# Dense mixture-of-experts dispatch: all loads ahead of the entry barrier, and four stores in place of five

## The chip, the cores and the metric

The kernel runs on one core of one Trainium2 chip. The metric is the time of one execution on the device in microseconds (us). The kernel before takes 92.71 us, the median of three runs (92.69 to 92.94). The profiled execution that is read below took 92.44 us, and its span, from the first recorded instruction to the last, is 90.7 us; times inside the kernel are counted from the start of that span.

## The reference

```python
batch, seq_len, d_model, n_experts = 8, 256, 512, 8
x             # (8, 256, 512) float32
gate_weights  # (8, 256, 8)   float32, not negative

def reference(x, gate_weights):
    gate_weights = gate_weights / (np.sum(gate_weights, axis=-1, keepdims=True) + 1e-8)
    output = x[:, :, None, :] * gate_weights[:, :, :, None]
    return output.astype(np.float32)
```

Each of the 2048 tokens has 512 numbers and 8 gate weights. The weights of a token are divided by their sum, and the token is written out eight times, each time multiplied by one of them. 4.19 MB of x and 0.07 MB of gates are read, 33.55 MB are written: the output is eight times as large as x.

## The kernel before

The 2048 tokens are laid out as 128 partitions with 16 tokens each (j from 0 to 15). So "a token" below means one j: 128 rows of 512 numbers for x, 128 rows of 8 x 512 numbers (16 KB in a partition) for the output. The results of one token fill one slot of a ring of ten slots; five stores, all issued by SyncE, write them out.

```python
SLOTS = 10
HEAD = 2
TAIL = 13
CHUNKS = ((0, 2, 0), (2, 3, 2), (5, 3, 5), (8, 4, 0), (12, 4, 6))   # first token, tokens, first slot

# ... issue_before_entry_barrier(nc, loads): moves the named loads to the front of their
#     engine's program, ahead of the barrier at which all engines meet at entry

    first_loads = [
        nc.sync.dma_start(out=g_all, in_=g_v),                                    # gates
        nc.scalar.dma_start(out=x_all[:, 0:HEAD, :], in_=x_v[:, 0:HEAD, :]),      # two tokens
    ]
    issue_before_entry_barrier(nc, first_loads)
    body_load = nc.sync.dma_start(
        out=x_all[:, HEAD:TAIL, :], in_=x_v[:, HEAD:TAIL, :]                      # eleven tokens
    )
    nc.sync.dma_start(out=x_all[:, TAIL:J, :], in_=x_v[:, TAIL:J, :])             # three tokens

    nc.vector.memset(warm, 0.0)
    nc.scalar.copy(out=warm, in_=warm)

    nc.vector.reduce_sum(out=gsum, in_=g_all, axis=mybir.AxisListType.X)
    nc.vector.tensor_scalar_add(out=gsum, in0=gsum, scalar1=1e-8)
    nc.vector.reciprocal(out=gsum, in_=gsum)
    nc.vector.tensor_tensor(
        out=gn, in0=g_all, in1=gsum.to_broadcast([P, J, E]), op=mult
    )

    # ... scale_one(engine, j, e, slot): one token times one gate, on ScalarE or VectorE (512 a partition)
    # ... scale_token(j, slot): one token times its eight gates, one VectorE instruction (4096 a partition)

    for j0, m, s0 in CHUNKS:
        for i in range(m):
            j, slot = j0 + i, s0 + i
            if j < 2:
                for e in range(E):
                    on_act = e < 3
                    scale_one(nc.scalar if on_act else nc.vector, j, e, slot)
            elif j == 2:
                for e in range(E):
                    scale_one(nc.scalar, j, e, slot)
            elif j == 3:
                for e in range(E):
                    scale_one(nc.scalar if e < 2 else nc.vector, j, e, slot)
            elif i == 0:
                for e in range(E):
                    scale_one(nc.scalar, j, e, slot)
            else:
                scale_token(j, slot)
        store = nc.sync.dma_start(
            out=out_v[:, j0 : j0 + m, :, :], in_=ring[:, s0 : s0 + m, :, :]
        )
        if j0 == 0:
            tc.add_manual_dep(
                store.ins,
                body_load.ins.name,
                # ...
                reason="no store among the loads",
            )
```

The slots 0 to 3 and 6 to 9 are used a second time, by the tokens 8 to 11 and 12 to 15: their scalings wait until the store that reads the slot has landed.

Of the kernel before, what the change touches and what calls it, by code (L numbers as in the profile page):

```python
# [1 line left out]

# [4 lines left out]

SLOTS = 10
HEAD = 2
TAIL = 13  # L10
CHUNKS = ((0, 2, 0), (2, 3, 2), (5, 3, 5), (8, 4, 0), (12, 4, 6))


def issue_before_entry_barrier(nc, loads):
    names = [bi.ins.name for bi in loads]

    def move(nc):
        blocks = nc.main_func.blocks
        entry = blocks[0].instructions
        moved = []  # L20
        for block in blocks[1:]:
            for ins in list(block.instructions):
                if ins.name in names:
                    block.instructions.remove(ins)
                    moved.append(ins)
        assert sorted(i.name for i in moved) == sorted(names)
        for ins in moved:
            at = next(k for k, other in enumerate(entry) if other.engine == ins.engine)
            entry.insert(at, ins)

    nc.at_finalize(move)


@with_exitstack
def kernel(
    ctx: ExitStack,
    tc: tile.TileContext,
    x: bass.AP,
    gate_weights: bass.AP,
    out: bass.AP,  # L40
):
    nc = tc.nc
    P = 128

    B, S, D = x.shape
    E = gate_weights.shape[-1]
    J = B * S // P

    fp32 = mybir.dt.float32
    mult = mybir.AluOpType.mult  # L50

    x_v = x.flatten_outer_dims().rearrange("(p j) d -> p j d", p=P)
    g_v = gate_weights.flatten_outer_dims().rearrange("(p j) e -> p j e", p=P)
    out_v = out.rearrange("b s e d -> (b s) e d").rearrange(
        "(p j) e d -> p j e d", p=P
    )

    pool = ctx.enter_context(tc.tile_pool(name="pool", bufs=1))

    g_all = pool.tile([P, J, E], fp32)  # L60
    x_all = pool.tile([P, J, D], fp32)
    ring = pool.tile([P, SLOTS, E, D], fp32)
    gsum = pool.tile([P, J, 1], fp32)
    gn = pool.tile([P, J, E], fp32)
    warm = pool.tile([P, 1], fp32)

    first_loads = [
        nc.sync.dma_start(out=g_all, in_=g_v),
        nc.scalar.dma_start(out=x_all[:, 0:HEAD, :], in_=x_v[:, 0:HEAD, :]),
    ]  # L70
    issue_before_entry_barrier(nc, first_loads)
    body_load = nc.sync.dma_start(
        out=x_all[:, HEAD:TAIL, :], in_=x_v[:, HEAD:TAIL, :]
    )
    nc.sync.dma_start(out=x_all[:, TAIL:J, :], in_=x_v[:, TAIL:J, :])

    nc.vector.memset(warm, 0.0)  # L77
    nc.scalar.copy(out=warm, in_=warm)  # L78
# [8 lines that stand above are left out]
    def scale_one(engine, j, e, slot):  # L87
        o_ap, s_ap = ring[:, slot, e, :], gn[:, j, e : e + 1]
        if engine is nc.scalar:
            nc.scalar.mul(out=o_ap, in_=x_all[:, j, :], mul=s_ap)  # L90
        else:
            nc.vector.tensor_scalar_mul(out=o_ap, in0=x_all[:, j, :], scalar1=s_ap)  # L92

    def scale_token(j, slot):
        nc.vector.tensor_tensor(  # L95
            out=ring[:, slot, :, :],
            in0=x_all[:, j : j + 1, :].to_broadcast([P, E, D]),
            in1=gn[:, j, :].unsqueeze(2).to_broadcast([P, E, D]),
            op=mult,
# [6 lines that stand above are left out]
                for e in range(E):  # L106
                    on_act = e < 3
                    scale_one(nc.scalar if on_act else nc.vector, j, e, slot)
            elif j == 2:
                for e in range(E):  # L110
                    scale_one(nc.scalar, j, e, slot)
            elif j == 3:
                for e in range(E):
                    scale_one(nc.scalar if e < 2 else nc.vector, j, e, slot)
            elif i == 0:
                for e in range(E):
                    scale_one(nc.scalar, j, e, slot)
            else:
                scale_token(j, slot)
        store = nc.sync.dma_start(  # L120
            out=out_v[:, j0 : j0 + m, :, :], in_=ring[:, s0 : s0 + m, :, :]
        )
        if j0 == 0:
            tc.add_manual_dep(
                store.ins,
                body_load.ins.name,
                mybir.DependencyInfo(
                    mybir.DependencyClass.Sync, mybir.DependencyReason.DATA
                ),
                reason="no store among the loads",  # L130
            )


# [1 line left out]
_INS = ['x', 'gate_weights']  # L135
_OUTS = [((8, 256, 8, 512), 'float32')]


# [23 lines left out]
```

## Time and profile before

| | |
|---|---|
| time, median of 3 runs | 92.71 us |
| span of the profiled execution | 90.7 us |
| VectorE busy | 46.7 us, 52% |
| ScalarE busy | 26.4 us, 29% |
| scaling of one token by one gate on ScalarE (40 of them) | 708 ns each |
| the same on VectorE (16) | 482 ns each |
| scaling of one token by all eight gates on VectorE (9) | 4420 ns each |
| mean rate of all transfers over the span | 417 GB/s |

A "busy" share is an average over the whole span, and its instructions overlap a little where they follow each other, so that ten VectorE scalings of 482 ns take 4.05 us. A transfer shows up in three places: the instruction that issues it, in the timeline of the issuing queue (some 0.35 us); its packets, which are moved by 16 DMA engines and are counted in the DMA row and by queue; and its landing, on which other instructions wait. The issuing queues of SyncE and ScalarE are called SPq and ACTq in the profile, and their packets are booked under q1 and q10. One packet is here one partition's part of a transfer.

### The profile page before, as it was taken

Reading aid. Unit: us, or ns where it says so; the run is one execution under the profiler, and the core shown is the slowest. Engines: PE = TensorE matmul, PEld = TensorE weight load, DVE = VectorE, ACT = ScalarE, POOL = GpSimd, SP = SyncE. Lnnn points to the kernel's source line nnn. Section 1 sums busy time; section 2 is a strip of 40 time slices with the busy share of each in tenths; the row PEclk is TensorE's granted clock in tenths of the full one; section 3 lists DMA queues with packets and bytes.
Section 4 is the critical chain, followed back from the end, with each engine's and each line's share of the span. In section 5 each row is a group of like instructions: output and inputs, shape, how many; then the busy total and the mean of one; then the engine's idle time right before and its main releaser. Section 6 shows DMA issues by size and latency. Waiting matters only on the chain.

```text
span 90.7 us, 140 instructions
## 1 busy us (share of the span) xinstructions
DVE 46.7 (52%) x30; ACT 26.4 (29%) x42; POOL 0.2 (0%) x4
## 2 busy tenths in 40 slices
DVE  0795399999999999999990495000000000000000
ACT  5393399997990000000000497000000000000000
POOL 0000000000000000000000000000000000000000
DMA  4998999999898889888988999999999982999990
GB/s 110 468 467 378 383 536 463 463 390 419 347 694 347 347 347 694 347 347 347 694 347 347 463 463 463 463 463 463 463 463 463 463 347 116 463 463 463 463 463 0
DMA packets 1296, 37.81 MB, mean 417 GB/s; under 512 B 144, under 2 KB 272, under 8 KB 528
## 3 DMA queue, kind: packets, MB, share of 16 engines
q1 hardware_dynamic: 1152, 37.29, 95.5%
q10 hardware_dynamic: 144, 0.52, 1.6%
HBM read 4.26 MB, written 33.55 MB: 417 GB/s over the span
## 4 chain that ended last, share of the span: by engine, by line
DMA 38%; DVE 17%; ACT 5%; ACTq 1%; issue 0%; SPq 0%
DMA out_dram<-ring 28%; DVE ring L95 14%; DMA x_all<-in_x_dram 11%; ACT ring L90 5%; DVE ring L92 3%; ACTq L157 1%; ACTq L90 0%; SPq L120 0%
## 5 line engine op out<-in xcount | busy, mean ns | idle before, releaser
L95 DVE TENSOR_TENSOR ring<-x_all,gn 128x4096 f32<-128x4096 f32 x9 | 39.2, 4420 | 3.5 <-DMA out_dram<-ring 3.5
L90 ACT ACTIVATE ring<-x_all,gn 128x512 f32<-128x512 f32 x40 | 24.9, 708 | 28.8 <-DMA out_dram<-ring 24.5
L92 DVE TENSOR_SCALAR ring<-x_all,gn 128x512 f32<-128x512 f32 x16 | 6.5, 482 | 2.8 <-DMA x_all<-in_x_dram 2.8
L78 ACT ACT_TABLE_LOAD x1 | 1.3, 1283 | 0.9 <-PEq L146 0.9
L80 DVE TENSOR_REDUCE gsum<-g_all 128x16 f32<-128x128 f32 x1 | 0.3, 286 | 1.6 <-DMA g_all<-in_gate_weights_dram 1.6
L77 DVE MEMSET warm<- 128x1 f32 x1 | 0.1, 59 | 1.0 <-PEq L146 1.0
L83 DVE TENSOR_TENSOR gn<-g_all,gsum 128x128 f32<-128x128 f32 x1 | 0.3, 291 | 0.0
L82 DVE RECIPROCAL gsum<-gsum 128x16 f32<-128x16 f32 x1 | 0.3, 252 | 0.0
L78 ACT COPY warm<-warm 128x1 f32<-128x1 f32 x1 | 0.2, 191 | 0.0
L81 DVE TENSOR_SCALAR gsum<-gsum 128x16 f32<-128x16 f32 x1 | 0.2, 176 | 0.0
L146 POOL MEMSET const-bfloat16-1.0<- 128x1 bf16 x1 | 0.1, 102 | 0.0
L146 POOL MEMSET const-uint8-127<- 128x1 uint8 x1 | 0.1, 102 | 0.0
L146 POOL MEMSET const-float32-0.0<- 128x1 f32 x1 | 0.1, 99 | 0.2 <-issue 0.2
L146 POOL MEMSET const-float32-1.0<- 128x1 f32 x1 | 0.1, 99 | 0.0
## 6 DMA issues: line engine op xcount, KB each, us to landing
out_dram<-ring SPq DMA_DIRECT2D x2, 6144.0 KB, 22.1
out_dram<-ring SPq DMA_DIRECT2D x1, 4096.0 KB, 11.5
x_all<-in_x_dram SPq DMA_DIRECT2D x1, 2816.0 KB, 9.6
x_all<-in_x_dram SPq DMA_DIRECT2D x1, 768.0 KB, 11.1
x_all<-in_x_dram ACTq DMA_DIRECT2D x1, 512.0 KB, 3.7
g_all<-in_gate_weights_dram SPq DMA_DIRECT2D x1, 64.0 KB, 2.6
out_dram<-ring SPq DMA_DIRECT2D x2, 28.1
```

The source lines that it names most:

```text
L77: nc.vector.memset(warm, 0.0)
L78: nc.scalar.copy(out=warm, in_=warm)
L80: nc.vector.reduce_sum(out=gsum, in_=g_all, axis=mybir.AxisListType.X)
L81: nc.vector.tensor_scalar_add(out=gsum, in0=gsum, scalar1=1e-8)
L82: nc.vector.reciprocal(out=gsum, in_=gsum)
L83: nc.vector.tensor_tensor(out=gn, in0=g_all, in1=gsum.to_broadcast([P, J, E]), op=mult)
L90: nc.scalar.mul(out=o_ap, in_=x_all[:, j, :], mul=s_ap)
L92: nc.vector.tensor_scalar_mul(out=o_ap, in0=x_all[:, j, :], scalar1=s_ap)
L95: nc.vector.tensor_tensor(out=ring[:, slot, :, :], in0=x_all[:, j : j + 1, :].to_broadcast([P, E, D]), in1=gn[:, j, :].unsqueeze(2).to_bro ...
L146: nc = _bacc.Bacc("TRN2", target_bir_lowering=False, num_devices=1)
L157: with _tile.TileContext(nc) as tc:
```

## The change

All three loads are now issued ahead of the entry barrier: first four tokens of x and then the other twelve from SyncE, and the gates from ScalarE. With every load issued before any store in the same queue, the explicit wait of the first store for the load of eleven tokens is dropped. The four stores have 2, 4, 4 and 6 tokens; the last reuses the slots 0 to 5. The work of the tokens 2 to 5 is dealt anew between the two engines, and ScalarE takes the tokens 6, 10, 11 and 12 whole. The aim is to have the engines that move the data supplied from the very beginning, with fewer and larger transfers, and never to let them run out between loads and stores.

```diff
-HEAD = 2
-TAIL = 13
-CHUNKS = ((0, 2, 0), (2, 3, 2), (5, 3, 5), (8, 4, 0), (12, 4, 6))
+HEAD = 4
+CHUNKS = ((0, 2, 0), (2, 4, 2), (6, 4, 6), (10, 6, 0))
 # ...
-        for ins in moved:
+        for ins in reversed(moved):
             at = next(k for k, other in enumerate(entry) if other.engine == ins.engine)
             entry.insert(at, ins)
 # ...
-    first_loads = [
-        nc.sync.dma_start(out=g_all, in_=g_v),
-        nc.scalar.dma_start(out=x_all[:, 0:HEAD, :], in_=x_v[:, 0:HEAD, :]),
-    ]
-    issue_before_entry_barrier(nc, first_loads)
-    body_load = nc.sync.dma_start(
-        out=x_all[:, HEAD:TAIL, :], in_=x_v[:, HEAD:TAIL, :]
-    )
-    nc.sync.dma_start(out=x_all[:, TAIL:J, :], in_=x_v[:, TAIL:J, :])
+    first_load = nc.sync.dma_start(out=x_all[:, 0:HEAD, :], in_=x_v[:, 0:HEAD, :])
+    gate_load = nc.scalar.dma_start(out=g_all, in_=g_v)
+    last_load = nc.sync.dma_start(out=x_all[:, HEAD:J, :], in_=x_v[:, HEAD:J, :])
+    issue_before_entry_barrier(nc, [first_load, gate_load, last_load])
 # ...
-            elif j == 2:
+            elif j < 6:
+                on_act = (8, 4, 0, 0)[i]
                 for e in range(E):
-                    scale_one(nc.scalar, j, e, slot)
-            elif j == 3:
-                for e in range(E):
-                    scale_one(nc.scalar if e < 2 else nc.vector, j, e, slot)
-            elif i == 0:
+                    scale_one(nc.scalar if e < on_act else nc.vector, j, e, slot)
+            elif j in (6, 10, 11, 12):
                 for e in range(E):
                     scale_one(nc.scalar, j, e, slot)
             else:
                 scale_token(j, slot)
-        store = nc.sync.dma_start(
+        nc.sync.dma_start(
             out=out_v[:, j0 : j0 + m, :, :], in_=ring[:, s0 : s0 + m, :, :]
         )
-        if j0 == 0:
-            tc.add_manual_dep(
-                # ... store.ins on body_load.ins.name, "no store among the loads"
-            )
```

More of the change, by code (lines that the diff above doesn't have):

```diff
@@ L119 @@
                 scale_token(j, slot)
-        store = nc.sync.dma_start(
+        nc.sync.dma_start(
             out=out_v[:, j0 : j0 + m, :, :], in_=ring[:, s0 : s0 + m, :, :]
         )
-        if j0 == 0:
-            tc.add_manual_dep(
[L125 to L130, printed above, removed]
-            )
 _INS = ['x', 'gate_weights']
```

## The prediction

> **What bounds the kernel now.** I read the page's second and third parts first, then the DMA issues, then SyncE's own waits, then the first microseconds of the timeline. The second part of the page (40 slices of 2.27 us each):
>
> ```profile
> DVE  0795399999999999999990495000000000000000
> ACT  5393399997990000000000497000000000000000
> ...
> DMA  4998999999898889888988999999999982999990
> ```
>
> The DMA row is full from the second slice to the last but one. VectorE and ScalarE have nothing to do after slice 25 of 40. The dips to 8 and 2 come from how whole packets are dealt to slices: counted packet by packet in the trace, all 16 DMA engines have work without a break from about 2.25 us on. The third part says how much there is:
>
> ```profile
> DMA packets 1296, 37.81 MB, mean 417 GB/s; under 512 B 144, under 2 KB 272, under 8 KB 528
> q1 hardware_dynamic: 1152, 37.29, 95.5%
> q10 hardware_dynamic: 144, 0.52, 1.6%
> ```
>
> 95.5% and 1.6% make 97.1% of 90.7 us, 88.0 us of packets for each of the 16 engines. q1 is SyncE's queue and q10 ScalarE's. The first data packet starts at 1.01 us and the last ends at 89.43 us, 88.42 us apart: only about 0.45 us per engine is idle in between, all of it in the ramp before 2.25 us. The other 2.3 us of the span are 1.0 ahead of the first packet and 1.2 behind the last one. So what the change can win is (a) part of 0.45 us, (b) per-packet costs; what it can lose is any gap that opens between the loads and the first store, or between two stores.
>
> Each store's margin is read from SyncE's waits, with the issues in the timeline at 10.60, 17.41, 26.08, 47.76 and 56.18 us:
>
> ```profile
> SPq L120 <- DVE ring L95: 43.5, 4, 21.3
> SPq L157 <- DMA out_dram<-ring: 33.1, 1, 33.1
> SPq L120 <- DMA x_all<-in_x_dram: 8.8, 1, 8.8
> ```
>
> Long as they are, these waits cost nothing: packets of the second store first move at 21.37 us, 4 us after its issue. The 8.8 us is the wait which the change removes: the first store's numbers are done at 7.96 us (ten VectorE scalings, 4.05 us from 3.91), but the store is held until the load of eleven tokens has landed.
>
> **What the Trainium skill says.** The Trainium skill, "DMA: Bandwidth & Descriptors", section "Issuing engines are not separate DMA queues": loads issued by SyncE and ScalarE run on the same 16 engines, and a second queue saves only issue time. The trace agrees: q1 and q10 fill one sum. Same page, "Queues, rings and completion order": each engine goes round-robin between rings, draining a whole packet of several descriptors from one before switching. This decides the case, and the trace agrees as far as it goes: the head of x (q10) and the eleven-token load (q1, issued at 0.91, so there from about 1.9) do not alternate. In the stretch 2.24 to 2.94 us all 66 packets are of q10, and packet by packet in the trace each of the 16 first packets of the eleven-token load starts 5 or 6 ns after one of q10's 16 completion packets:
>
> ```profile
> DMA packets 66, 0.27 MB, mean 386 GB/s; under 512 B 0, under 2 KB 0, under 8 KB 66
> ...
> q10 hardware_dynamic: 66, 0.27, 95.9%
> ```
>
> So a transfer once begun on an engine is finished there (eight packets and a completion) before the other queue has its turn. "Where 436 GB/s comes from" on the same page gives 435.2 GB/s over 16 ports, 27.2 for one; the trace's 65,536-byte packets take 2418 ns, 27.1 GB/s. A faster engine is not to be had.
>
> **The change part by part.** Packet times first, from the trace's medians: 6,144 bytes 234 ns and 22,528 bytes 836 ns, so 0.0367 ns a byte plus 8.3 ns. (Check: 4,096 bytes gives 159, measured 159; 65,536 gives 2416, measured 2418.)
>
> *Bytes and packets.* Every engine serves 8 partitions. Before: gates 8 x 27, head 8 x 159, eleven tokens 8 x 836, three tokens 8 x 234, stores 8 x 1213, 16 x 1815, 16 x 2418 = 87.5 us; measured 88.0, the rest being slow first reads (about 0.4 us above the medians in the loads) and completion packets. After: gates 8 x 27 = 0.22; four tokens, 8,192 bytes, 8 x 309 = 2.48; twelve tokens, 24,576 bytes, 8 x 911 = 7.29; stores 9.70, 38.69, and for six tokens (98,304 bytes a partition, which I take to go as two packets of 49,152) 16 x 1815 = 29.04: 87.4 us. Saved: 0.06, and with two completion packets fewer about 0.08. Fewer stores bring nothing, since they were queued end to end.
>
> *Ahead of the barrier.* The twelve-token load is issued right behind the first (issue takes 0.33 to 0.42 us each) and is in the ring long before the four tokens are through. The first transfer has 309 ns packets in place of 27 ns gates, so engines do not run dry while the rest of the descriptors arrive: I give 0.2 of the 0.45 us ramp. The barrier itself comes some 0.4 us later, because SyncE reaches it later; ScalarE's table load then ends at 2.6 in place of 2.2 us, still ahead of the gates.
>
> *The start of the compute: later.* Now the gates stand behind four tokens. In the kernel before, the head's completion packets fall between 2.94 and 3.48 us after about 1.7 us of work on an engine, so engines effectively began at 1.24 to 1.78. After: 2.48 for the four tokens, 0.2 slow reads, 0.23 gates, so the gates' last packet at 4.15 to 4.7 us. From last packet to reader took 0.37 us (2.23 to the reduction at 2.61), so the reduction starts at about 5.05; the four small VectorE operations take 1.30 (2.61 to 3.91), then 4.05 for ten scalings: 10.4 us in place of 7.96.
>
> *The first store.* Issue 10.4, in place of 10.60; from issue to first packets 1.0 to 1.5 us (the gates' load before: issued 0.00, packets from 1.01 on): 11.4 to 11.9. Loads are gone from the engines at 1.24 to 1.78 + 2.9 + 7.3 + 0.1 = 11.55 to 12.1. So the removed wait gives nothing: the numbers arrive just as the loads run out. I expect a gap of 0 to 0.4 us, 0.1 in the mean.
>
> *The later stores.* Each is due when the one ahead drains. From 11.6: 21.3, 40.7 and 60.0 us, end near 89.1. Second store: VectorE does four scalings of token 3 (to 12.0), waits for the twelve tokens (about 12.0), does 16 for tokens 4 and 5 at 0.41 each (2.47 for 6): 18.6, packets at 19.6, 1.7 us to spare. ScalarE needs twelve at 0.62 (11.14 for 18), done at 17.5. Third: three whole tokens at 4.37 (13.01 for 3, with hand-over): 31.7, 8 to spare. Last: slots 2 to 5 come free when the second store lands at 41; three tokens on VectorE end at 54.4, packets at 55.4, 4.6 to spare. ScalarE has three tokens there, 5.0 us each, two of them long before.
>
> Sum: -0.1 packets, -0.2 ramp, +0.1 gap ahead of the first store: 92.71 - 0.2 = 92.5 us.
>
> **Rivals.** *Gates starved.* If an engine drains both x loads of SyncE's ring before it turns to ScalarE's, the gates arrive at 12.2 us instead of 5.05; the first store's packets then start at about 18.6 to 19.1, some 7 us after the loads are gone: 99.4 us. For it: both x loads are in one ring, and the trace shows no case where two transfers of one ring competed with one of another. Against: the round-robin of the Trainium skill's page, and in the trace the switch to q10 at the end of the gates' transfer. About one in twelve. *A gap ahead of the first store.* The margin worked out is nothing, and its terms (start of engines, slow first reads, issue to first packet) are uncertain by some 0.3 us each; 0.5 to 1.0 us of gap makes 93.0 to 93.5. *The second store late.* Its margin of 1.7 us is the smallest of the later ones; a late landing of the twelve tokens eats it one for one, but the same delay also pushes the first store's drain, so 93 at most. *All of the ramp won.* If gates and four tokens fill the engines at once and no gap opens, 0.45 + 0.1 + some 0.3 of slow reads are saved: 91.9. More than 2% (below 90.9) can't come from anything listed, as 37.81 MB stay.
>
> **Range and chances.** The sum is 92.5; the ramp and the gap give 91.9 to 93.4 eight times in ten, the upper side wider for the gap. Faster by over 2% 0.01; slower by over 2% (above 94.6) only by starved gates or a gap of over 2 us: 0.10; within 2% 0.89.
>
> **What would show it.** In the profile after: the reduction (L80 before) starting near 5 us shows the order of the queues; near 12 us, starvation. First store issued at 10.4. Bandwidth slices from the second on without a hole near 12 us (slice 5) and near 21 us. Sum of both queues about 87.8 us. Last store issued near 54.5. I am wrong if DMA slices have a hole after slice 1, or if the six-token store's packets are slower per byte than the others.

## Result: 92.22 us, half a per cent faster

The kernel after takes 92.22 us (median of 6 runs, 92.10 to 92.33), the kernel before 92.70 us in the same comparison; the ratio is 0.9946 with a 95% interval of 0.9931 to 0.9961. The change is a real gain of 0.5 us, well inside the 2% band. The prediction said 92.5 us with a range of 91.9 to 93.4.

The page of the kernel after, second and third part (40 slices of 2.26 us; packets, megabytes and share of 16 engines by queue):

```profile
DVE  0059989999999900006999991000000000000000
ACT  4219999999999920006950000000000000000000
...
DMA  5999999999999999867999999988998899889980
...
DMA packets 1136, 37.81 MB, mean 418 GB/s; under 512 B 112, under 2 KB 240, under 8 KB 240
q1 hardware_dynamic: 992, 37.75, 97.1%
q10 hardware_dynamic: 144, 0.07, 0.2%
```

The DMA row is again full from the second slice on. There is no hole at slice 5 or 6, where the first store follows the loads, nor at slice 9 or 10, where the second store follows the first. The 8, 6 and 7 further on are, as in the kernel before, whole packets dealt to slices; no work is missing there (0.00 us in the table below). VectorE and ScalarE start their scalings at 6.45 us, some 2.5 us or a good slice later than before. 97.3% of the 90.5 us span are 88.1 us of packets per engine, as much as before.

The timeline of the kernel after, its first 20 us (start, duration, both in us; lines left out):

```profile
0.00 0.39 SPq L66 DMA_DIRECT2D x_all<-in_x_dram  x1
0.12 0.38 ACTq L67 DMA_DIRECT2D g_all<-in_gate_weights_dram  x1
...
0.44 0.42 SPq L68 DMA_DIRECT2D x_all<-in_x_dram  x1
...
5.30 0.29 DVE L74 TENSOR_REDUCE gsum<-g_all 128x16 f32<-128x128 f32 x1 [3.90 <-DMA g_all<-in_gate_weights_dram]
...
6.45 5.63 DVE L86 TENSOR_SCALAR ring<-x_all,gn 128x512 f32<-128x512 f32 x14
10.58 44.57 SPq L112 DMA_DIRECT2D out_dram<-ring  x4
12.48 6.42 DVE L86 TENSOR_SCALAR ring<-x_all,gn 128x512 f32<-128x512 f32 x16 [0.40 <-DMA x_all<-in_x_dram]
```

The reduction of the gates starts at 5.30 us (2.61 before), since the gates now share the engines with four tokens of x, and yet the first store is issued at 10.58 us, where it was issued at 10.60 before. Packet by packet in the trace, the engines end the twelve tokens between 11.43 and 12.05 us and begin the first store at most 36 ns later, most of them after 2 or 3: no gap.

SyncE's own waits in the kernel after (us in total, times, longest):

```profile
SPq L112 <- DVE ring L89: 35.0, 2, 22.4
SPq L140 <- DMA out_dram<-ring: 34.4, 2, 28.9
SPq L112 <- DVE ring L86: 17.3, 2, 9.3
```

The wait of 8.8 us for the load is gone, and a wait of 9.3 us for VectorE's scalings has taken its place.

Counted over the packets of both traces, in us per engine:

| | before | after |
|---|---|---|
| first packet starts / last packet ends | 1.01 / 89.43 | 1.02 / 89.36 |
| sum of packets | 88.02 | 88.15 |
| without work, from the first packet to 4 us | 0.44 | 0.24 |
| without work, 4 to 85 us | 0.01 | 0.00 |

So these two executions differ by 0.1 us only (92.44 and 92.33 us), a fifth of the gain in the medians. The other four fifths had to be looked for in runs.

### The profile page after: what moved, and what is told of

It reads as the page before. It is cut to its first block, busy times and chain, and to the rows that moved or that the text cites. A ratio compares the mean times of both kernels' runs of the same rounds, so it can differ in the third digit from the quotient of the medians.

```text
span 90.5 us, 154 instructions
## 1 busy us (share of the span) xinstructions
DVE 39.2 (43%) x41; ACT 32.3 (36%) x52; POOL 0.2 (0%) x4
## 4 chain that ended last, share of the span: by engine, by line
DMA 38%; DVE 17%; DVEq 5%; SPq 0%; issue 0%
DMA out_dram<-ring 25%; DMA x_all<-in_x_dram 13%; DVE ring L89 10%; DVE ring L86 7%; DVEq L140 5%; SPq L66 0%; DVEq L89 0%; SPq L112 0%
## 5 line engine op out<-in xcount | busy, mean ns | idle before, releaser
L84 ACT ACTIVATE ring<-x_all,gn 128x512 f32<-128x512 f32 x50 | 30.8, 709 | 13.0 <-DMA out_dram<-ring 9.3
L89 DVE TENSOR_TENSOR ring<-x_all,gn 128x4096 f32<-128x4096 f32 x6 | 26.2, 4420 | 9.7 <-DMA out_dram<-ring 9.7
L86 DVE TENSOR_SCALAR ring<-x_all,gn 128x512 f32<-128x512 f32 x30 | 12.1, 481 | 0.4 <-DMA x_all<-in_x_dram 0.4
```

The lines of the kernel that those rows point to most:

```text
L89: nc.vector.tensor_tensor(out=ring[:, slot, :, :], in0=x_all[:, j : j + 1, :].to_broadcast([P, E, D]), in1=gn[:, j, :].unsqueeze(2).to_bro ...
```

## Experiments

Each was timed in five rounds beside the kernel before; the median of that kernel was 92.71 us in the first group of four runs, 92.59 in the second and 92.65 in the third. Its times reach from 92.39 to 94.89 us; the ratios and counts below leave out, on both sides, executions more than 1.5% above the fastest of the same kernel. Theory A was that the gain is at the start; theory B that it comes from four stores in place of five.

### The kernel before, against itself

No edit.

> The kernel before, timed against itself: what two medians differ by when nothing is changed. All theories: ratio 1.000, interval within 0.998 to 1.002; span 90.6 to 90.9 us. If its spans scatter by more than 0.3 us, then the gain of 0.5 us can't be read from one pair of traces.

92.78 us, ratio 0.9994 (0.9965 to 1.0024). So a single comparison resolves some 0.3%, less finely than expected, and the gain of 0.5% stands out of it; but its executions scatter by 0.9 us, so one pair of traces can't show where 0.5 us went. The profile of this run (93.33 us) is worth more than its time. Its loads are slower on one engine: one packet of the eleven tokens took 1,585 ns in place of 836, that engine had the eleven tokens at 11.16 us, the other 15 by 10.13. The first store waits for all 16, and so it is issued at 11.66 in place of 10.60 us. SyncE's wait, the issues and the packets in the stretch 11.85 to 12.50 us of this run:

```profile
SPq L120 <- DMA x_all<-in_x_dram: 9.9, 1, 9.9
...
11.66 45.83 SPq L120 DMA_DIRECT2D out_dram<-ring  x5
...
DMA packets 12, 0.03 MB, mean 47 GB/s; under 512 B 7, under 2 KB 7, under 8 KB 12
```

Nearly nothing moves there. On 15 engines the three tokens that were to cover the wait are through by 12.14 us and the store's first packet starts at 12.51; 0.66 us per engine, in the mean of all 16, are without work between 4 and 20 us, where the trace read for the prediction had 0.01. But the late engine doesn't stand still. Its packets follow each other without a pause: it ends its three tokens at 13.01 us, when the store is already there, and the last store at 90.33, after all others (90.10 to 90.29). So the lag of this one engine sets the time, and the wait that it prolonged costs the other 15 time which they did not need.

### One half of the change each

Loads only: the kernel after with the old five stores and the old dealing of the tokens.

```diff
-CHUNKS = ((0, 2, 0), (2, 4, 2), (6, 4, 6), (10, 6, 0))
+CHUNKS = ((0, 2, 0), (2, 3, 2), (5, 3, 5), (8, 4, 0), (12, 4, 6))
 # and the branches of the loop as in the kernel before
```

> The loads of the kernel after (four and twelve tokens from SyncE, gates from ScalarE, all ahead of the barrier, no added wait) with the five stores and the dealing of the kernel before. Theory A (the gain is at the start: engines run dry less in the ramp): the whole gain, 92.2 us, ratio 0.994 to 0.996. Theory B (the gain comes from four stores in place of five): no gain, 92.7 us, ratio 0.999 to 1.001.

92.22 us, ratio 0.9924 (0.9897 to 0.9952): the whole gain.

Stores only: the kernel before with the four stores and the new dealing; its loads and its wait stay.

```diff
-CHUNKS = ((0, 2, 0), (2, 3, 2), (5, 3, 5), (8, 4, 0), (12, 4, 6))
+CHUNKS = ((0, 2, 0), (2, 4, 2), (6, 4, 6), (10, 6, 0))
 # and the branches of the loop as in the kernel after
```

> The four stores and the dealing of the kernel after with the loads and the wait of the kernel before. Theory A (gain at the start): 92.7 us, ratio 0.999 to 1.001; second store issued near 18.8 us, 2.5 us before the first one has drained, so no gap. Theory B (gain from four stores in place of five): 92.2 us, ratio 0.994 to 0.996.

92.52 us, ratio 0.9977 (0.9955 to 0.9999): some 0.2 us, at the edge of what the comparison resolves, and it does not add to that of the loads, as both halves together give 92.22 too. Theory B falls. The gain is in the loads.

### Which part of the loads: the dropped wait

The wait put back into the kernel after:

```diff
+        if j0 == 0:
+            tc.add_manual_dep(store.ins, last_load.ins.name, ...)   # first store after the twelve tokens
```

> The kernel after with the dropped wait put back: the first store is issued when the load of twelve tokens has landed. My theory: in the kernel before, this wait was covered by the load of three tokens behind the one waited for (1.9 us of work on each engine); here nothing stands behind it, so the engines run dry from 11.4 to 12.0 us until 1.0 to 1.5 us after an issue near 12.45: a gap of 1.5 to 2.2 us, 93.8 to 94.4 us, ratio 1.012 to 1.018. Rival (the wait is hidden as it was before): 92.2 us.

94.00 us (93.88 to 94.06), ratio 1.0111 (1.0065 to 1.0158), 1.8 us more than the kernel after. The timeline and, below, the packets in the stretch 11.97 to 13.27 us:

```profile
12.43 6.80 SPq L112 DMA_DIRECT2D out_dram<-ring  x2
...
DMA packets 0, 0.00 MB, mean 0 GB/s; under 512 B 0, under 2 KB 0, under 8 KB 0
```

The store is issued when the last load has landed, and its first packets start 0.84 us later, at 13.27. For 1.3 us not one packet moves on the 16 engines, and per engine 1.61 us are lost between 4 and 20 us. So the drop of the wait is a condition of the new loads, in which nothing stands behind the twelve tokens.

Now the wait dropped from the kernel before:

```diff
-        if j0 == 0:
-            tc.add_manual_dep(store.ins, body_load.ins.name, ...)
```

> The kernel before without the wait of the first store for the load of eleven tokens, nothing else changed. My theory: that wait was hidden. The first store is issued at 8.0 in place of 10.6 us, its packets still start near 11.7 us behind the loads, and the time is that of the kernel before, 92.7 us, ratio 0.998 to 1.001. Rival (the wait cost part of the gain): 92.2 to 92.4 us.

94.20 us (93.80 to 95.42), ratio 1.0163 (1.0124 to 1.0202): slower by 1.6 us, against both expectations. The queue is full, and yet less gets through. Both traces between 9.70 and 12.90 us, first the kernel before:

```profile
DMA packets 177, 1.34 MB, mean 420 GB/s; under 512 B 32, under 2 KB 32, under 8 KB 160
...
q1 hardware_dynamic: 177, 1.34, 100.2%
```

Then the kernel before without the wait:

```profile
7.96 50.84 SPq L120 DMA_DIRECT2D out_dram<-ring  x5
...
DMA packets 119, 0.65 MB, mean 203 GB/s; under 512 B 16, under 2 KB 16, under 8 KB 118
...
q1 hardware_dynamic: 119, 0.65, 85.9%
```

The packets that start in this stretch fill 86% of it in place of all, and carry half as much. The store is issued at 7.96 us, but its first packet starts at 12.91, behind the loads as expected. What changes is the load in front of it: of the 128 packets of the three tokens (6,144 bytes, 234 ns), half take 300 to 794 ns. Their sum per engine is 3.06 us in place of 1.89. A store that stands in the queue slows the load ahead of it, which the next two runs test. That was what the wait had been for; in the source it is commented "no store among the loads". The scatter of the kernel before has not gone with the wait: two of the five executions counted lie over 0.6 us above the fastest. In the profiled one (94.62 us) a late engine again ends its loads at 14.31 us, the others by 13.55, and the last store at 91.62, the others by 90.87.

### How early is too early

Is it the small packets of the third load, or the store? The eleven and the three tokens joined to one load of fourteen, without the wait:

```diff
-TAIL = 13
+TAIL = 16
-    nc.sync.dma_start(out=x_all[:, TAIL:J, :], in_=x_v[:, TAIL:J, :])
 # and the wait of the first store dropped
```

> The kernel before without the wait of the first store, and with the loads of eleven and three tokens joined to one of fourteen: the first store is still issued near 8 us, some 4 us before the loads are through. Theory R (an engine that has a store queued behind a load slows its last load packets, whatever their size): loads slowed by about as much as in the run without the wait, some 1.2 us per engine, 93.8 to 94.4 us. Rival (it needs a further transfer of small packets between the running load and the store, here gone): packets of the fourteen tokens at their usual rate, 92.5 to 92.8 us.

93.71 us (93.63 to 94.78), ratio 1.0102 (1.0040 to 1.0165), just under the range that the theory gave. The store's issue in the timeline:

```profile
8.04 50.70 SPq L119 DMA_DIRECT2D out_dram<-ring  x5
```

In the trace the first six packets of the fourteen tokens on each engine take their usual 1,062 ns, most of them exactly, the seventh mostly 1,550 to 2,250 and the eighth 1,230 to 1,760; together 9.98 us per engine where eight at 1,062 are 8.50, and 1.28 of the 1.48 us lie in the last two. The rival falls: small packets are not needed. The time alone doesn't measure the stretch, for the fourth store's numbers come late too, and there 0.85 us per engine are without work.

The same asked of the kernel after: its first store cut into two of one token each, so that a store is issued 2 us earlier.

```diff
-CHUNKS = ((0, 2, 0), (2, 4, 2), (6, 4, 6), (10, 6, 0))
+CHUNKS = ((0, 1, 0), (1, 1, 1), (2, 4, 2), (6, 4, 6), (10, 6, 0))
```

> The kernel after with its first store of two tokens cut into two of one token each, so that the first is issued near 8.5 instead of 10.6 us, 3 us before the loads are through. Theory R (a store queued early slows the last packets of the load ahead of it): packets of the twelve tokens above 912 ns, 92.8 to 93.4 us. Rival (a store queued behind a load in progress does it no harm): 92.2 to 92.3 us, all packets of the twelve tokens at 912 ns.

93.31 us (93.09 to 93.57), ratio 1.0060 (1.0042 to 1.0078): 1.1 us slower than the kernel after. Its timeline and the packets between 9.60 and 13.10 us:

```profile
8.51 2.33 SPq L112 DMA_DIRECT2D out_dram<-ring  x2
13.40 0.88 DVE L86 TENSOR_SCALAR ring<-x_all,gn 128x512 f32<-128x512 f32 x2 [1.41 <-DMA x_all<-in_x_dram]
...
DMA packets 73, 1.20 MB, mean 342 GB/s; under 512 B 16, under 2 KB 16, under 8 KB 16
...
q1 hardware_dynamic: 73, 1.20, 102.8%
```

Engines fully occupied, at 342 GB/s. Six packets of the twelve tokens take 912 ns on all engines, the seventh 912 to 1,264, the eighth 1,429 to 1,794: 0.81 us more per engine. In the kernel after, with the store issued at 10.58 us, all 128 take 912. So three runs show it for three kinds of loads (+1.17, +1.28, +0.81 us per engine). It hits the last packets of the load, those that start 0.8 us or more after the store's issue. Why they stretch isn't shown.

### Which part of the loads: order and barrier

The twelve tokens issued behind the barrier:

```diff
-    issue_before_entry_barrier(nc, [first_load, gate_load, last_load])
+    issue_before_entry_barrier(nc, [first_load, gate_load])
+    last_load = nc.sync.dma_start(out=x_all[:, HEAD:J, :], in_=x_v[:, HEAD:J, :])
```

> The kernel after with the load of twelve tokens behind the entry barrier instead of ahead of it. By my theory the four tokens keep each engine busy until about 4.2 us and the twelve are issued at 0.9 us, in the ring by 2 us: no gap, 92.2 us, ratio to the kernel before 0.994 to 0.996, and the barrier is passed 0.36 us earlier without effect. Rival (the early issue of all loads is the gain): 92.5 to 92.7 us.

92.23 us (92.11 to 92.44), ratio 0.9952 (0.9934 to 0.9970): as the kernel after. The four tokens keep the engines busy long enough; that the twelve go ahead of the barrier as well brings nothing.

The kernel before with its two early loads exchanged between the queues, so that x comes first:

```diff
-        nc.sync.dma_start(out=g_all, in_=g_v),
-        nc.scalar.dma_start(out=x_all[:, 0:HEAD, :], in_=x_v[:, 0:HEAD, :]),
+        nc.scalar.dma_start(out=g_all, in_=g_v),
+        nc.sync.dma_start(out=x_all[:, 0:HEAD, :], in_=x_v[:, 0:HEAD, :]),
```

> The kernel before with the two loads ahead of the barrier exchanged between the queues: the two tokens of x from SyncE, the gates from ScalarE; wait, five stores and the other loads as they were. Theory A2 (the gain of the change is that x and not the gates reaches the engines first): 92.2 to 92.35 us, ratio 0.994 to 0.996, and few runs above 92.8. Rival (the gain needs the four and twelve tokens and the dropped wait): 92.6 to 92.75 us, with as many runs above 93 us as the kernel before has.

92.75 us, ratio 0.9991 (0.9961 to 1.0022): no gain in the median, so the order of the first two loads alone is not the gain. The single executions say more. Of the 17 counted, 8 are faster than the fastest of the kernel before in this group (92.25 to 92.43 against 92.45 us), which is the 0.2 us of the ramp; 5 take 93.08 us or more, so the slow tail of the kernel before is still there.

The kernel after with the gates first, all from SyncE:

```diff
-    first_load = nc.sync.dma_start(out=x_all[:, 0:HEAD, :], in_=x_v[:, 0:HEAD, :])
-    gate_load = nc.scalar.dma_start(out=g_all, in_=g_v)
+    gate_load = nc.sync.dma_start(out=g_all, in_=g_v)
+    first_load = nc.sync.dma_start(out=x_all[:, 0:HEAD, :], in_=x_v[:, 0:HEAD, :])
 # last_load as before; issued ahead of the barrier in the order gates, four tokens, twelve tokens
```

> The kernel after with the gates as the first load in SyncE's own queue, ahead of both loads of x; ScalarE's queue is not used. Theory A (big packets first fill the ramp): engines run dry in the first microsecond as in the kernel before, 92.4 to 92.7 us, though the reduction starts at 2.6 in place of 5.3 us and the first store is issued 2.5 us earlier. Rival (what counts is that everything is issued ahead of the barrier): 92.2 us, unchanged.

93.15 us (92.73 to 93.75), ratio 1.0054 (1.0024 to 1.0084): 0.9 us slower than the kernel after, more than I gave it. x's first packet starts at 1.53 in place of 1.02 us, and 0.56 us per engine are without work up to 4 us (0.24 in the kernel after); that is 0.3. The rest is one engine: it ends the four tokens at 5.47 us, the others by 4.94; one packet of its twelve tokens takes 0.4 us too long; it ends the last store at 90.47, the others by 89.65. Nothing lets an engine catch up, as each has the same packets to move. Why it was slow isn't shown.

The gates last, behind both loads of x in SyncE's queue:

```diff
-    issue_before_entry_barrier(nc, [first_load, gate_load, last_load])
+    issue_before_entry_barrier(nc, [first_load, last_load, gate_load])   # gate_load now from nc.sync
```

> The kernel after with the gates as the third load in SyncE's own queue, behind the twelve tokens; this is the starvation that the prediction's first rival feared, made on purpose. By the prediction's working: reduction near 12.2 to 12.5 us, first store issued near 17.7, engines without work for some 7 us, 99.2 to 99.6 us, ratio 1.07. If the compute behind the start were not what sets the first store, it would stay at 92.2 us.

99.16 us (98.99 to 99.25), ratio 1.0704 (1.0677 to 1.0732). The timeline and the packets in the stretch 12.10 to 18.40 us:

```profile
12.37 0.29 DVE L74 TENSOR_REDUCE gsum<-g_all 128x16 f32<-128x128 f32 x1 [10.50 <-DMA g_all<-in_gate_weights_dram]
...
17.65 0.35 SPq L112 DMA_DIRECT2D out_dram<-ring  x1
...
DMA packets 0, 0.00 MB, mean 0 GB/s; under 512 B 0, under 2 KB 0, under 8 KB 0
```

This is the hole of some 7 us which the prediction feared, in size and in place: 6.89 us per engine are without work between 4 and 20 us.

### An attempt to beat both

What is left in the kernel after up to 4 us is 0.24 us per engine without work. So I let both queues bring x at once, two tokens each, with the gates behind the second half in ScalarE's queue:

```diff
-    first_load = nc.sync.dma_start(out=x_all[:, 0:HEAD, :], in_=x_v[:, 0:HEAD, :])
+    first_load = nc.sync.dma_start(out=x_all[:, 0:2, :], in_=x_v[:, 0:2, :])
+    second_load = nc.scalar.dma_start(out=x_all[:, 2:HEAD, :], in_=x_v[:, 2:HEAD, :])
 # gate_load and last_load as before; second_load, too, is issued ahead of the barrier, before the gates
```

> The kernel after with its first load cut in two, tokens 0 and 1 from SyncE and 2 and 3 from ScalarE ahead of the gates, so that both queues bring x at once. If what is left at the start is that some engines get their first packet 0.3 to 0.7 us after the others: up to 0.15 us less, 92.05 to 92.2 us. If the slow first reads are what is left: no gain, 92.2 to 92.4 us.

99.65 us (99.51 to 99.85), ratio 1.0722 (1.0671 to 1.0772). A far miss, and an instructive one. The wait for the gates in this run, and its packets between 5.00 and 11.50 us:

```profile
DVE gsum L75 <- DMA g_all<-in_gate_weights_dram: 11.1, 1, 11.1
...
DMA packets 223, 2.81 MB, mean 432 GB/s; under 512 B 0, under 2 KB 111, under 8 KB 111
...
q1 hardware_dynamic: 112, 2.75, 98.2%
q10 hardware_dynamic: 111, 0.06, 2.9%
```

In 6.5 us, 112 packets of one queue and 111 of the other: the engines take from both queues in turn, packet by packet. Each gate packet of 27 ns waits for one of 912. An engine has eight of each, and so the gates land when the twelve tokens do. In the kernel after, the same turns are taken, between 2.40 and 4.10 us:

```profile
DMA packets 154, 0.70 MB, mean 412 GB/s; under 512 B 0, under 2 KB 73, under 8 KB 73
...
q1 hardware_dynamic: 81, 0.66, 92.0%
q10 hardware_dynamic: 73, 0.04, 7.2%
```

There the partners of the gates are packets of the four tokens, 309 ns each, and the gates are through at 4.8 us. No run beat the kernel after; loads only and the run with the twelve tokens behind the barrier equal it.

## Why the prediction was right, and where it was not

**The bound: right.** The engines that move the data set the time in every run, and what a run lost beside the kernel after is found in its trace as engines without work, or with stretched packets, between 4 and 20 us, or as one engine that lags (in the run with fourteen tokens also at its fourth store).

**The first store arrives as the loads run out: right.** Predicted were the reduction at 5.05 us, the issue at 10.4 and the loads gone between 11.55 and 12.1 us; measured 5.30, 10.58 and 11.43 to 12.05. The gap given 0.1 us is 0.00. From issue to first packet I took 1.0 to 1.5 us from the gates' load; the runs with a bare store show 0.84 (12.43 to 13.27).

**The later stores: right.** The second is issued at 19.00 us (18.6 predicted), its packets start at 21.2; the last is issued at 54.8 (54.5 predicted). There is no hole at any hand-over.

**The ramp: right in size.** 0.2 of 0.44 us predicted, 0.44 to 0.24 in the pair of traces.

**The packets: not quite.** Instead of 0.1 us less the sum is 0.13 more (88.15). The term that was mis-sized is the slow first reads: above its median the load of four tokens spends 0.53 us per engine, not the 0.2 that I allowed.

**"A transfer once begun on an engine is finished there": wrong.** The engines change queues after each packet, as the last two views show; the Trainium skill, "DMA: Bandwidth & Descriptors", section "Queues, rings and completion order", speaks of a whole packet of several descriptors, and here one partition's part of a transfer was the unit. That the head of x and the eleven tokens did not alternate in the kernel before must have another cause, which is open. The gates' landing came out right all the same, because the last gate packet follows the last of four tokens either way. That the wrong picture cost the prediction nothing was luck; it did lead to the attempt that ended at 99.65 us.

**The size of the gain: 0.2 us predicted, 0.5 measured.** The result lies in the range, but the sum was read from one execution, one of the fastest of the kernel before (92.44 us). Its missing term is not the wait. "The removed wait gives nothing" agrees with both traces of the kernel before. Where no hole opens ahead of the first store, the end follows the engine that ends its loads last:

| execution | last engine ends its loads | last packet of all ends | us between |
|---|---|---|---|
| kernel before, 92.44 us | 12.02 | 89.43 | 77.4 |
| kernel before, 93.33 us | 13.01 | 90.33 | 77.3 |
| stores only, 92.53 us | 12.27 | 89.58 | 77.3 |
| before without the wait, 94.62 us | 14.31 | 91.62 | 77.3 |
| kernel after, 92.33 us | 12.05 | 89.36 | 77.3 |
| loads only, 92.24 us | 11.99 | 89.31 | 77.3 |
| twelve behind the barrier, 92.44 us | 11.90 | 89.38 | 77.5 |
| kernel after with the wait, 94.02 us | 11.97 | 91.08 | 79.1 |

The stores' packets alone are 9.70 + 29.04 + 38.69 = 77.4 us on each engine. So in the first seven the engine that was last at the loads went on without a wait; only in the eighth did a wait cost time.

What the change gains is the ramp, 0.2 us, and, as far as the record goes, rarer late engines. Of the 107 executions of the kernel before that were counted, 30 took 92.8 us or more. Of 35 of the kernels after, loads only and twelve behind the barrier none took more than 92.44. In the traces of these three not one packet of the twelve tokens took longer than 912 ns; of the 128 packets of the eleven tokens 10 were stretched in the execution of 92.44 us (from 836 to at most 1,202 ns) and 27 in that of 93.33 (to at most 1,585). The prediction had this term, as "some 0.3 of slow reads" in its rival "All of the ramp won", and left it out of the sum. On the mean engine nothing of it was saved (88.15 us of packets). Neither x first with the old loads nor four and twelve tokens behind the gates does without late engines. This is argued from counts and traces: why packets stretch with one set of loads and not with another stays open, and so does a rest, as even the fastest executions are 0.3 us apart (92.39 and 92.10), 0.1 more than the ramp.

**A condition that I had not seen.** The drop of the wait is only harmless because the gates come late: the scalings then end at 10.5 us, when the loads have about one packet per engine to go. A store issued at 8.5 us would have cost 1.1 us, one at 12.4 us 1.8.

**Starved gates: priced right.** 99.4 us worked out, 99.16 measured when the gates were put last. What protects the kernel after is not ScalarE's queue as such but that the gates take turns with the four tokens.

## What to carry to other kernels

Where the transfers are the bound, aim the first store at the moment when the loads run out: too late leaves the engines empty, and too early stretches the last packets of the load ahead of it. A small load in a second queue lands after as many packets of the first queue as it has itself, so pair it with short ones. And before a wait is blamed in which 15 engines stand idle, look at the sixteenth: where each has the same packets to move, the one that ends its loads last sets the time, and one execution doesn't show how late that can be.

## What the runs showed of the hardware that was not expected

- Two queues are served in turn, one packet each: 112 and 111 packets in 6.5 us, though the one kind takes 912 ns and the other 27.
- A store queued behind a load slows that load's last packets, with the engines busy all the time: 234 ns packets to as much as 790, 912 to as much as 1,794, some 0.8 to 1.3 us per engine in three runs.
- First reads are slow: the load of four tokens took 3.01 us per engine in the kernel after where eight packets at the median of 309 ns are 2.48.
- An engine that lags early lags to the end, where nothing holds the others back: 0.8 us behind them at the last store when the gates came first. From the last load packet on any engine to the last store packet it took 77.3 to 77.5 us in seven traces, with a late engine or without.
